# Depthwise convolution wholly on TensorE inside the first projection, with DMA-delayed copies

## The chip, the cores and the metric

The kernel runs on one core of one Trainium2 chip. The metric is device time in microseconds (us) of one execution, lower being better; several executions give a median. A core has TensorE (PE, matmuls), VectorE (DVE), ScalarE (ACT) and GpSimd (POOL), each working through its own instructions in order, and SyncE (SP), which here issues the loads. ACT and POOL can issue transfers too. All transfers share 16 DMA engines.

## The reference

Two layers of a streaming encoder on one sequence of 256 tokens, width 2048, in float32. Each layer has a token mixer (a Conformer convolution module in layer 0, gated linear attention in layer 1) and then a conv-FFN of hidden width 5632. Shift, scale and gate of every sub-layer come from a vector c by a projection (adaLN).

```python
mod = (silu(c) @ ada_w[i] + ada_b[i]).reshape(B, 6, 1, D)
h = rms_norm(x, norm_g[i, 0]) * (1.0 + scale_m) + shift_m
# layer 0's mixer:
a, gate = split(h @ w_in, 2)
z = causal_dwconv(a * sigmoid(gate), dw_w, dw_b)      # 31 taps per channel
y = silu(layer_norm(z, ln_g, ln_b)) @ w_out
x = x + gate_m * rms_norm(y, norm_g[i, 1])
```

The six parts of mod are numbered m = 0 to 5: shift, scale and gate of the mixer, then of the FFN. The change touches layer 0's mixer and the adaLN work that runs beside it.

## The kernel before, in words

**Weights.** All weights arrive as 1 MB blocks (128 partitions by 2048 numbers) in the order of one list, `items`, through a class `Stream`. It issues the loads on SP's queue, up to eight items ahead (L92 to L99), into two pools of four buffers: `raw` for weights and `cols` for the adaLN blocks marked early. A weight block is split into a high part in a reduced float format (hi, on ACT, L121) and the remainder (lo, on DVE, L123), in halves of 1024 columns. Each product is then three matmuls: hi by high input, hi by low input, lo by high input.

**adaLN blocks.** A block comes in one of two forms. A column block (`ada_col`, L353) is multiplied with silu(c) on PE: four float32 matmuls of 512 columns, in four column tiles of 32 beside each other, which the profile shows as eight records a block. After four blocks DVE transposes the sums and small matmuls with a mask add the four partial sums (adas, L378). A row block (`ada_row`, L347) holds the same matrix transposed, and one DVE instruction multiplies it with cb, silu(c) on all partitions, and adds up along the row (L350). The tables `ADA`, `COLS_CONV`, `COLS_COUT` and `ROWS_COUT` say after which weight block how many adaLN blocks stand in the list.

**The mixer's first half** (`conv_mixer`, L597 on). The projection runs in six steps (`STEPS`), each over some input tiles and some of the 16 output blocks j of 128 channels, since input tiles become ready only as shift and scale arrive. Numbered from 1: steps 5 and 6 are the last ones, for which all input tiles are ready; step 5 completes blocks 0 to 7, two for each weight block, and step 6 completes blocks 8 to 15, one each. `gather` (L658) adds up the steps' sums in the tile pair (L665), and once a block is complete takes the gate's sigmoid on ACT (L668) and multiplies (L671).

**The convolution.** Eight blocks are convolved on DVE, one instruction for each of 30 taps (`taps_dve`, L685). The other eight, `PE_BLOCKS`, go to PE (`taps_pe`). There the four 32-channel groups of a block are copied with delays of 0 to 3 frames into a tile zr by matmuls with pieces of the identity (ps_late, L713) and copies on ACT (L715). Then 8 times 4 matmuls with 32 by 32 diagonals, held in a tile zt, give the 31 taps (L730); zt is built by a DVE product (L724) and by 16 ACT instructions (L728). The function `conv` hands out both kinds in small portions after the projection, with early column blocks between them (the loop with `early_cols`). `mean_add` and `squares` sum blocks for the layer norm by matmuls with ones (acc_m, L644; acc_v, L633).

**Layer norm and the second half.** The variance is turned into r_ln on DVE and ACT (L778 to L786), all 16 blocks are centred (L789), then scaled, passed through Silu and split (L792 to L796). `proj_out` multiplies by the output weights in four quarters of 512 columns (ps_cout, L525 to L527). Its evacuation multiplies by the gate, which `gate_rows` writes to DRAM as one row and reads back on all partitions, on POOL's queue (L511, L515). The gate's m = 2 has to be complete for that. m = 3 and 4 are wanted by the FFN behind it.

## Time and profile before

| | us |
|---|---|
| median of three runs | 2382.68 (2380.72 to 2386.43) |
| the profiled execution | 2384.22 |
| its span, first to last instruction | 2382.5 |
| PE busy in the span | 2326.0 |
| DVE busy | 1776.0 |
| ACT busy | 1225.2 |
| the output projection's first matmul starts at | 371.17 |

The span runs from the first to the last instruction of the profiled execution. Times inside it count from its start. A group of instructions is named by line, engine, operation and the tiles that it writes and reads. A release such as "<-DMA raw<-in_adac" names what the engine waited for last.

### The profile page before, as it was taken

The page shows a single profiled execution, that of the slowest core. Times are in us where ns is not written, and L with a number is a line of the kernel's source. Part 1 is how long each engine was busy: PE and PEld are TensorE (multiplying, and loading weights), DVE is VectorE, ACT ScalarE, POOL GpSimd, SP SyncE. Part 2 cuts the span into 40 slices and gives each one's busy share as a digit, 9 for nine tenths or more (in the row PEclk, how much of TensorE's full clock was granted, in tenths as well). Part 3 has the DMA queues.
Part 4 walks back from the last instruction along what each step waited for, and adds up shares of the span by engine and source line. Part 5 has one row for each costly group of instructions (what it writes and reads, how often), then busy time and mean ns, then how long its engine had stood idle before and what let it go on. Part 6 is the DMA issues. An engine that isn't in the chain of part 4 may idle for free.

```text
span 2382.5 us, 34222 instructions
## 1 busy us (share of the span) xinstructions
PE 2326.0 (98%) x13522; PEld 1957.6 (82%) x13522; DVE 1776.0 (75%) x2522; ACT 1225.2 (51%) x1941; POOL 16.7 (1%) x43
## 2 busy tenths in 40 slices
...
GB/s 385 342 312 300 303 245 296 261 206 280 281 306 358 303 287 302 364 290 298 350 166 259 287 213 228 164 228 109 289 288 264 198 192 194 186 187 195 193 200 118
DMA packets 86578, 609.31 MB, mean 256 GB/s; under 512 B 10064, under 2 KB 10128, under 8 KB 13456
## 3 DMA queue, kind: packets, MB, share of 16 engines
...
HBM read 604.94 MB, written 2.13 MB: 255 GB/s over the span
## 4 chain that ended last, share of the span: by engine, by line
PE 95%; DMA 2%; ACT 1%; DVE 1%; issue 0%; SPq 0%; DVEq 0%; ACTq 0%
PE ps_fb L410 14%; PE ps_fa L410 14%; PE ps_fa L412 7%; PE ps_fb L412 7%; PE ps_fo L526 6%; PE ps_fo L527 6%; PE ps_fo L525 6%; PE ps_cin L756 3%; PE ps_cin L758 3%; PE ps_cin L757 3%; PE ps_r L410 2%; PE ada L364 2%; PE ps_r L412 1%; PE ps_q L410 1%; PE ps_cout L525 1%; PE ps_k L410 1%
## 5 line engine op out<-in xcount | busy, mean ns | idle before, releaser
L123 DVE TENSOR_TENSOR lo<-raw,hi 128x1024 fp32r<-128x1024 f32 (+1 forms) x760 | 914.0, 1214 | 392.0 <-ACT hi L121 388.6
L121 ACT CAST hi<-raw 128x1024 fp32r<-128x1024 f32 (+1 forms) x760 | 784.2, 1042 | 802.9 <-PE ps_fa L410 187.3
L410 PE MATMUL ps_fa<-h,hi 128*128 128x512 f32 x1408 | 358.6, 393 | 1.0 <-ACT h L486 0.9
L410 PE MATMUL ps_fb<-h,hi 128*128 128x512 f32 x1408 | 357.2, 392 | 0.0
L350 DVE CUSTOM_DVE_ANT_0 raw<-raw,cb 128x2048 f32<-128x2048 f32 x140 | 319.6, 2285 | 28.8 <-DMA raw<-in_adar 28.4
L410 PEld LDWEIGHTS ps_fa<-h,hi 128*128 128x128 f32 x1408 | 253.6, 189 | 46.8 <-issue 1.2
L410 PEld LDWEIGHTS ps_fb<-h,hi 128*128 128x128 f32 x1408 | 253.6, 189 | 44.2
L526 PE MATMUL ps_fo<-lo,u 128*128 128x512 f32 x704 | 274.7, 390 | 3.6 <-DVE lo L123 3.6
L527 PE MATMUL ps_fo<-hi,u 128*128 128x512 f32 x704 | 274.5, 390 | 0.0
L525 PE MATMUL ps_fo<-hi,u 128*128 128x512 f32 x704 | 273.9, 390 | 0.0
L412 PEld LDWEIGHTS ps_fa<-h,lo 128*128 128x128 f32 x1408 | 194.1, 190 | 14.9 <-DVE lo L123 0.5
L412 PEld LDWEIGHTS ps_fb<-h,lo 128*128 128x128 f32 x1408 | 193.8, 190 | 14.1
L412 PE MATMUL ps_fa<-h,lo 128*128 128x256 f32 x1408 | 198.9, 282 | 0.1
L412 PE MATMUL ps_fb<-h,lo 128*128 128x256 f32 x1408 | 198.2, 282 | 0.0
L526 PEld LDWEIGHTS ps_fo<-lo,u 128*128 128x128 f32 x704 | 132.6, 188 | 31.4 <-DVE lo L123 4.0
L527 PEld LDWEIGHTS ps_fo<-hi,u 128*128 128x128 f32 x704 | 132.6, 188 | 27.7
L525 PEld LDWEIGHTS ps_fo<-hi,u 128*128 128x128 f32 x704 | 132.5, 188 | 27.3
L756 PE MATMUL ps_cin<-h,hi 128*128 128x256 f32 x512 | 147.1, 291 | 6.1 <-ACT hi L121 6.1
L758 PE MATMUL ps_cin<-h,lo 128*128 128x256 f32 x512 | 144.6, 288 | 2.3 <-DVE lo L123 2.3
L757 PE MATMUL ps_cin<-h,hi 128*128 128x256 f32 x512 | 145.9, 288 | 0.4 <-DVE h L491 0.4
L756 PEld LDWEIGHTS ps_cin<-h,hi 128*128 128x128 f32 x512 | 99.3, 195 | 18.5 <-ACT hi L121 8.8
L757 PEld LDWEIGHTS ps_cin<-h,hi 128*128 128x128 f32 x512 | 99.6, 195 | 5.6 <-DVE h L491 4.7
...
## 6 DMA issues: line engine op xcount, KB each, us to landing
raw<-in_fin SPq DMA_DIRECT2D x176, 1024.0 KB, 4.8
raw<-in_adar SPq DMA_DIRECT2D x140, 1024.0 KB, 6.0
raw<-in_fout SPq DMA_DIRECT2D x88, 1024.0 KB, 5.6
raw<-in_adac SPq DMA_DIRECT2D x44, 1024.0 KB, 6.1
raw<-in_gin SPq DMA_DIRECT2D x33, 1024.0 KB, 4.9
raw<-in_cin SPq DMA_DIRECT2D x32, 1024.0 KB, 11.0
raw<-in_cout SPq DMA_DIRECT2D x16, 1024.0 KB, 7.2
raw<-in_gv SPq DMA_DIRECT2D x16, 1024.0 KB, 4.8
```

What stands on the lines that cost most here:

```text
L121: nc.scalar.copy(hi[:, :w], r[:, s : s + w])
L123: nc.vector.tensor_sub(lo[:, :w], r[:, s : s + w], hi[:, :w].bitcast(F32))
L350: V.tensor_tensor_reduce(out=r, in0=r, in1=cb, scale=1.0, scalar=0.0, op0=ALU.mult, op1=ALU.add, accum_out=mod[l, m][:, k : k + 1])
L364: nc.tensor.matmul(ps[32 * (j % 4) : 32 * (j % 4) + 32], cz[:, kt], r[:, j * n : (j + 1) * n], start=kt < 4, stop=kt >= KT - 4, tile_posit ...
L410: nc.tensor.matmul(ps, hi(k * P), act[k], start=k == 0, stop=False)
L412: nc.tensor.matmul(ps[:, :T], lo(k * P), act[k][:, :T], start=False, stop=k == nk - 1)
L525: nc.tensor.matmul(pv, ah, wh, start=kt == 0, stop=False)
L526: nc.tensor.matmul(pv, ah, wl, start=False, stop=False)
L527: nc.tensor.matmul(pv, al, wh, start=False, stop=kt == nk - 1)
L756: nc.tensor.matmul(ps[:, b], hi(o), ah, start=k == 0, stop=False)
L757: nc.tensor.matmul(ps[:, b], hi(o), al, start=False, stop=False)
L758: nc.tensor.matmul(ps[:, b], lo(o), ah, start=False, stop=k == nk - 1)
```

## The change

All 16 blocks are convolved on PE, inside projection steps 5 and 6. When a block is complete, `gather` writes it to DRAM from POOL's queue and reads it back four times, delayed by 0 to 3 frames, straight into one of three zr tiles. The delaying matmuls and the ACT copies go, and so do the DVE taps. `conv` now does one whole block; it is called as soon as more than `LAG` = 2 blocks wait. Both halves of zt are built on DVE.

The adaLN list changes: of m = 2 only 4 blocks stay columns and of m = 4 only 8 (`COLS`), the rest become row blocks; 25 of these stand inside the projection, where 12 column blocks stood, and four column blocks (`gap_cols`, where 16 stood in the tail) lie at its end, ahead of the output weights. In the output projection stand 8 column and 11 row blocks (4 and 16 before). Column blocks there are ordered behind a matmul of the output projection, row blocks of layer 0 behind the layer norm.

The start loads in another order: column blocks between the halves of x, cb behind the first weight block, part of the parameters early by ACT's queue and the rest late, the taps in step 3 and half as many. The layer norm becomes one fixed line of DVE instructions with high priority, in which each block's product, low part and the centring of a later block alternate, and the Silu table is loaded only after the root.

What moves, on three engines. First PE at the end of the projection, before: the last projection matmuls (ps_cin), a column block (ada), the mean sums (acc_m), then the delaying matmuls (ps_late) and diagonals (ps_conv) of the first block for PE.

```order
1616 L757 MATMUL ps_cin_15_2789<-h_15_1828,hi_1024_2720 128x256
1617 L758 MATMUL ps_cin_15_2789<-h_15_1828,lo_1024_2721 128x256
1618 L364 MATMUL ada_2630<-raw_2470,cz 32x512 x4
1619 L644 MATMUL acc_m_2867<-pair_301,ones 128x256
1620 L644 MATMUL acc_m_2867<-pair_316,ones 128x256
1621 L713 MATMUL ps_late_0_2872<-zp_176,ident 32x284 x4
1622 L713 MATMUL ps_late_1_2878<-zp_176,ident 32x284 x4
1623 L713 MATMUL ps_late_2_2884<-zp_176,ident 32x284 x4
1624 L713 MATMUL ps_late_3_2890<-zp_176,ident 32x284 x4
1625 L730 MATMUL ps_conv_2896<-zr,zt 32x256 x8
```

Now the first convolution stands in step 5, between the projections of blocks 2 and 3 (ps_cin_2, ps_cin_3), and PE comes to it directly after block 2.

```order
1093 L719 MATMUL ps_cin_2_2001<-h_15_1842,hi_0_1905 128x256
1094 L720 MATMUL ps_cin_2_2001<-h_15_1842,hi_0_1905 128x256
1095 L721 MATMUL ps_cin_2_2001<-h_15_1842,lo_0_1906 128x256
1096 L694 MATMUL ps_conv_2036<-zr_181,zt 32x256 x32
1097 L719 MATMUL ps_cin_3_2074<-h_12_1822,hi_1024_1909 128x256
1098 L720 MATMUL ps_cin_3_2074<-h_12_1822,hi_1024_1909 128x256
1099 L721 MATMUL ps_cin_3_2074<-h_12_1822,lo_1024_1910 128x256
1100 L719 MATMUL ps_cin_3_2074<-h_13_1827,hi_1024_1909 128x256
```

So PE cannot go on to block 3 before block 0's zr has landed. Second POOL's queue at that place, now (before, it issues nothing there): the writes of blocks 0 and 1 (zd, from pair), the four reads of each into zr, then the write of block 2.

```order
16 L678 DMA zd_1942<-pair_305 128x256 [waits DVE_49]
17 L678 DMA zd_1977<-pair_320 128x256 [waits DVE_49]
18 L680 DMA zr_181<-zd_1942 32x4x256 [waits DMASW0_49,Pool_49]
19 L680 DMA zr_181<-zd_1942 32x4x255
20 L680 DMA zr_181<-zd_1942 32x4x254
21 L680 DMA zr_181<-zd_1942 32x4x253
22 L680 DMA zr_182<-zd_1977 32x4x256 [waits DMASW1_49,Pool_49]
23 L680 DMA zr_182<-zd_1977 32x4x255
24 L680 DMA zr_182<-zd_1977 32x4x254
25 L680 DMA zr_182<-zd_1977 32x4x253
26 L678 DMA zd_2030<-pair_335 128x256 [waits DMASW2_49,DVE_49]
```

The reads wait for the write's landing (DMASW), and a later block's write stands behind an earlier block's reads. Third DVE in step 5, before: the additions of blocks 0 to 2 (pair from ps_cin), two low parts, the gate products (pair from g), and then taps.

```order
168 L665 TENSOR_TENSOR pair_301<-pair_301,ps_cin_0_1897 128x512
169 L665 TENSOR_TENSOR pair_316<-pair_316,ps_cin_1_1927 128x512
170 L123 TENSOR_TENSOR lo_0_1975<-raw_1706,hi_0_1974 128x1024
171 L123 TENSOR_TENSOR lo_1024_1979<-raw_1706,hi_1024_1978 128x1024
172 L671 TENSOR_TENSOR pair_301<-pair_301,g 128x256
173 L671 TENSOR_TENSOR pair_316<-pair_316,g 128x256
174 L665 TENSOR_TENSOR pair_331<-pair_331,ps_cin_2_1982 128x512
175 L685 SCALAR_TENSOR_TENSOR pair_301<-pair_301,tp 128x255
```

And now, at the same place:

```order
179 L669 TENSOR_TENSOR pair_305<-pair_305,ps_cin_0_1913 128x512
180 L669 TENSOR_TENSOR pair_320<-pair_320,ps_cin_1_1948 128x512
181 L355 ISA raw_1720,m_105<-raw_1720,cb 128x2048
182 L355 ISA m_105 128x1
183 L675 TENSOR_TENSOR pair_305<-pair_305,g 128x256
184 L675 TENSOR_TENSOR pair_320<-pair_320,g 128x256
185 L669 TENSOR_TENSOR pair_335<-pair_335,ps_cin_2_2001 128x512
186 L355 ISA raw_1722,m_105<-raw_1722,cb 128x2048
```

A row block (raw with cb) stands ahead of the gate product that the first write to DRAM waits for.

The diff, cut to what the prediction speaks of:

```diff
-PE_BLOCKS = (5, 7, 9, 11, 12, 13, 14, 15)
-NA = 12
+LAG = 2
+NA = 10
...
-ADA = ((2, 1, 1, 0), (3, 3, 2, 0), (1, 1, 1, 1, 1, 1, 1, 1), (3, 3, 2, 0), (1,) * 4, (1,) * 8)
-COLS_CONV = 16
+ADA = ((2, 1, 1, 0), (3, 3, 2, 0), (1, 1, 2, 1, 2, 1, 2, 1), (3, 3, 2, 0), (2, 3, 3, 2), (2, 2, 2, 2, 2, 1, 1, 0))
+COLS = {2: (0, 4), 4: (8, 16)}
...
-COLS_COUT = (0, 0, 0, 1), (1, 1, 1, 1), (1, 1, 0, 0), (0, 0, 0, 0)
-ROWS_COUT = (0, 0, 0, 4), (2, 1, 2, 1), (2, 1, 2, 1), (0, 0, 0, 0)
+COLS_COUT = (0, 0, 0, 0), (1, 1, 1, 1), (1, 1, 1, 1), (0, 0, 0, 0)
+ROWS_COUT = (0, 0, 0, 1), (1, 1, 2, 1), (2, 1, 1, 1), (0, 0, 0, 0)
...
+    pr = const.tile([P, NPAR], F32, tag="pr", name="pr")
+    A.dma_start(out=pr[:, :C_DWB], in_=par[:, :C_DWB])
...
-    cols += [(0, m, k, 4, i) for m in (2, 4) for k in range(0, KT, 4) for i in range(4)]
-    rows += [(0, 3, k) for k in range(KT)]
+    cols += [(0, m, k, 4, i) for m in (2, 4) for k in range(*COLS[m], 4) for i in range(4)]
+    rows += [(0, m, k) for m in (2, 3, 4) for k in range(KT) if m == 3 or not COLS[m][0] <= k < COLS[m][1]]
...
-            for _ in range(ADA[s][i]):
-                if ada:
+            for a in range(ADA[s][i]):
+                if ada and (s < 2 or s == 3 or s == 2 and a == 0):
                     put(ada.pop(0))
                 else:
-                    fillc(1)
-    early_cols = list(cols[:COLS_CONV])
-    fillc(COLS_CONV)
+    gap_cols = list(cols[:4])
+    fillc(4)
...
     def ada_row(key, r):
         _, l, m, k = key
-        V.tensor_tensor_reduce(out=r, in0=r, in1=cb, scale=1.0, scalar=0.0, op0=ALU.mult, op1=ALU.add,
-                               accum_out=mod[l, m][:, k : k + 1])
+        with tc.issue_after(apool["ln"].ins) if "ln" in apool and l == 0 else ExitStack():
+            V.tensor_tensor_reduce(out=r, in0=r, in1=cb, scale=1.0, scalar=0.0, op0=ALU.mult, op1=ALU.add,
+                                   accum_out=mod[l, m][:, k : k + 1])
...
-                             start=kt < 4, stop=kt >= KT - 4, tile_position=(0, 32 * (j % 4)))
+            with tc.issue_after(apool["tok"].ins) if "tok" in apool else ExitStack():
+                nc.tensor.matmul(ps[32 * (j % 4) : 32 * (j % 4) + 32], cz[:, kt], r[:, j * n : (j + 1) * n],
+                                 start=kt < 4, stop=kt >= KT - 4, tile_position=(0, 32 * (j % 4)))
         if i == KT // per - 1:
...
     for t in range(2):
+        st.load(t + 2)
         for c in range(4):
             nc.sync.dma_start(out=X[t][c], in_=x[t, :, c * 512 : (c + 1) * 512])
-    nc.sync.dma_start(out=pr, in_=par)
-    st.load(4)
+    st.load(5)
+    nc.sync.dma_start(out=cb, in_=cvec.to_broadcast([P, D]))
+    nc.sync.dma_start(out=pr[:, C_DWB:], in_=par[:, C_DWB:])
...
-            nc.sync.dma_start(out=tp, in_=taps)
+            tp = cm.tile([P, KT, 4, 8], F32, tag="tp", name="tp", bufs=1)
             ss = new_sums("in")
+            for zr in zrs:
+                G.memset(zr, 0.0)
...
+                    for i in added[len(squared) :][: 3 if n < KT - 1 else KT]:
                         squares(i)
...
             def gather(j, ps, last):
...
                     V.tensor_mul(zp, zp, g)
+                    zr = zrs[j % 3]
+                    zd = dram.tile([4, 32, T], F32, tag="zd", name=f"zd{j}", bufs=3)
+                    G.dma_start(out=zd.rearrange("b n t -> (b n) t"), in_=zp)
+                    for i in range(4):
+                        G.dma_start(out=zr[32 * i : 32 * i + 32, :, 28 + i :], in_=zd.rearrange("b n t -> n b t")[:, :, : T - i])
+                    on_pe.append(j)
...
-            def taps_dve():
...
-                            V.scalar_tensor_tensor(z[:, s:], zp[:, : T - s], tap(j, s), z[:, s:], ALU.mult, ALU.add)
-                            yield None
-                    for j, _, _ in two:
-                        yield j
...
-            def taps_pe():
...
-                        pr4 = pp["ps"].tile([P, 512], F32, tag="ps", name=f"ps_late{j}_{b}")[:, : 28 + T]
-                        for i in range(4):
-                            nc.tensor.matmul(pr4[32 * i : 32 * i + 32], ident[:, 32 * b : 32 * b + 32], zp[:, 4 - i : 32 + T - i],
-                                             start=True, stop=True, tile_position=(0, 32 * i))
-                        A.copy(zr[:, b], pr4)
-                        yield None
...
-                            else:
-                                for b in range(16):
-                                    A.activation(zt[:, b // 4, b % 4], mask32, AF.Copy, scale=w[:, a + b // 4, b % 4 : b % 4 + 1])
...
+            def conv():
...
+                j = on_pe.pop(0)
+                ps = pp["ps"].tile([P, 2 * T], F32, tag="ps", name=f"ps_conv{j}")[:, :T]
+                for a in range(8):
+                    if a % 4 == 0:
+                        zt = cm.tile([P, 4, 4, 32], F32, tag="zt", name="zt", bufs=2)
+                        V.tensor_mul(zt, tp[:, j, :, a : a + 4].rearrange("p b a -> p a b").unsqueeze(3).to_broadcast([P, 4, 4, 32]),
+                                     mask32.unsqueeze(1).unsqueeze(1).to_broadcast([P, 4, 4, 32]))
                     for b in range(4):
+                        nc.tensor.matmul(ps[32 * b : 32 * b + 32], zt[:, a % 4, b], zrs[j % 3][:, b, 28 - 4 * a : 28 - 4 * a + T],
+                                         start=a == 0, stop=a == 7, tile_position=(0, 32 * b))
+                A.activation(zs[j], ps, AF.Identity, bias=pc(C_DWB + j))
+                return j
...
             for s, (k0, nk, j0, j1) in enumerate(STEPS):
+                if s == 2:
+                    nc.sync.dma_start(out=tp.rearrange("p j b a -> p (j b a)"), in_=taps)
...
                         gather(j, ps, k0 + nk == KT)
-                    if k0 + nk == KT:
-                        conv(dve, taps_dve, 8)
+                        if len(on_pe) > LAG:
+                            z = conv()
+                            for i in done:
+                                mean_add(i)
+                            done[:] = [z]
...
-            for step in range(1000):
-                if step < len(early_cols):
-                    st.upto(("col",) + early_cols[step], False)
-                if len(added) == KT:
-                    break
-                late, ready[:] = list(ready), []
...
-                conv(pe, taps_pe, 7)
-                conv(dve, taps_dve, 8)
+            st.prepare(2)
+            while on_pe:
+                z = conv()
...
+                done[:] = [z]
...
-            V.scalar_tensor_tensor(part_a, acc["m"], 1.0 / D, part_a, ALU.mult, ALU.add)
-            V.tensor_add(mu, mean_a, part_a)
-            A.activation(part_a, part_a, AF.Square)
-            V.scalar_tensor_tensor(r, acc["v"], 1.0 / D, part_a, ALU.mult, ALU.subtract)
-            V.tensor_scalar_max(r, r, 0.0)
-            A.activation(r, r, AF.Sqrt, bias=epsb)
-            V.reciprocal(r, r)
-            warm(AF.Silu, acc["v"])
-            for j in range(KT):
-                V.tensor_sub(zs[j], zs[j], mu)
...
+            line = []
+            def queue(f, *args):
+                with tc.issue_after(line[-1].ins) if line else ExitStack():
+                    line.append(f(*args))
+            def center(j):
+                if j < KT:
+                    queue(V.tensor_sub, zs[j], zs[j], mu)
+            def low(j):
+                if j >= 0:
+                    queue(V.tensor_sub, us[j][:, T:], zs[j], us[j][:, :T].bitcast(F32))
+            with tc.high_priority(SPLIT_FIRST):
+                queue(V.scalar_tensor_tensor, part_a, acc["m"], 1.0 / D, part_a, ALU.mult, ALU.add)
+                queue(V.tensor_add, mu, mean_a, part_a)
+                A.activation(part_a, part_a, AF.Square)
+                queue(V.scalar_tensor_tensor, r, acc["v"], 1.0 / D, part_a, ALU.mult, ALU.subtract)
+                queue(V.tensor_scalar_max, r, r, 0.0)
+                A.activation(r, r, AF.Sqrt, bias=epsb)
+                warm(AF.Silu, r)
+                for j in range(3):
+                    center(j)
+                queue(V.reciprocal, r, r)
+                for j in range(KT):
+                    queue(V.tensor_mul, zs[j], zs[j], r)
+                    A.activation(zs[j], zs[j], AF.Silu, bias=pc(C_LNB + j), scale=pc(C_LNG + j))
+                    us.append(hpool.tile([P, 2 * T], F32R, tag="h", name=f"uc{j}"))
+                    A.copy(us[j][:, :T], zs[j])
+                    low(j - 2)
+                    center(j + 3)
+                low(KT - 2)
+                low(KT - 1)
+            st.upto(("col",) + gap_cols[-1], False)
...
```

101 lines of the change are left out of this document (23 added, 78 removed).

## The prediction

> **What bounds the kernel now.** I read the page first. TensorE (PE) is busy for 98% of the span, so a change counts where it takes work off PE's queue or closes one of PE's few gaps.
>
> ```profile
> PE 2326.0 (98%) x13522; PEld 1957.6 (82%) x13522; DVE 1776.0 (75%) x2522; ACT 1225.2 (51%) x1941; POOL 16.7 (1%) x43
> ```
>
> Next a table of the first layer's mixer by stretch. Its columns are the stretch, its length, the busy time of PE, weight loads, DVE, ACT and POOL, PE's clock, the DMA share and GB/s.
>
> ```profile
> 0.00:30.00 30.00, 10.34 (x89) 5.01 (x89) 5.16 (x19) 14.96 (x36) 1.50 (x12) 0.98 0.95 379
> 30.00:185.00 155.00, 150.03 (x1240) 132.16 (x1241) 110.96 (x142) 61.35 (x84) 0.00 (x0) 0.97 0.84 344
> 185.00:269.80 84.80, 84.80 (x708) 72.62 (x707) 77.14 (x152) 36.48 (x53) 0.00 (x0) 1.00 0.73 291
> 269.80:356.10 86.30, 86.14 (x1048) 48.34 (x1048) 83.38 (x209) 51.17 (x184) 1.33 (x1) 1.00 0.76 268
> 356.10:371.20 15.10, 1.97 (x9) 0.31 (x9) 15.10 (x39) 7.46 (x14) 2.14 (x4) 0.62 0.61 158
> 371.20:462.00 90.80, 90.33 (x408) 71.58 (x409) 76.25 (x85) 46.51 (x71) 0.00 (x0) 0.99 0.86 334
> ```
>
> These are the start, projection steps 1 to 4, steps 5 and 6, the convolution tail, layer norm, and the output projection. PE idles 20 us in the start and 13 us in layer norm, and is full nearly everywhere else. Third, the chain of waits in order of time (start, length, what), which tells what holds those two places.
>
> ```profile
> 26.96 0.84 ACT zt L728 x4
> ...
> 28.92 0.94 ACT hi L121
> ...
> 29.91 0.58 PE ps_cin L756
> ...
> 199.12 0.99 PE ada L364 x8
> ...
> 318.75 3.16 PE ps_conv L730 x56
> 321.91 0.86 PE ada L364 x8
> ...
> 355.06 1.01 PE ada L364 x4
> 356.08 13.10 DMA raw<-in_adac
> 369.23 1.94 PE ada L364 x8
> 371.17 0.73 PE ps_cout L525
> ```
>
> The first projection matmul waits for a weight cast (hi) that stands on ACT behind diagonals for a convolution that comes 240 us later (zt). The gap ahead of the output projection is booked to a late adaLN block.
>
> **Start.** Three transfers no longer stand ahead of the first weight block:
>
> ```profile
> cb<-in_cvec ACTq DMA_DIRECT2D x1, 1024.0 KB, 4.8
> ...
> tp<-in_taps SPq DMA_DIRECT2D x1, 504.0 KB, 11.5
> pr<-in_par SPq DMA_DIRECT2D x1, 366.0 KB, 5.6
> ```
>
> They hold 1.9 MB, of which about 0.16 MB of parameters stay early: 1.8 MB at the 379 GB/s of the first row of the table is 4.7 us. The zt work on ACT goes as well (0.84 us on the chain and a little more). I take -6. The bounds are 0, since the second half of x now comes behind three column blocks and may end last, and -8.
>
> **Column blocks out of the projection.** Twelve of them leave PE between projection blocks, at 0.99 us each (the row at 199.12), with three sums of about 0.3: -13. Row blocks on DVE replace them. These groups price that and what follows (line, engine, operation, shapes, count, busy time, mean ns):
>
> ```profile
> L123 DVE TENSOR_TENSOR lo<-raw,hi 128x1024 fp32r<-128x1024 f32 x96 | 113.7, 1219 | 18.6 <-ACT hi L121 18.6
> ...
> L350 DVE CUSTOM_DVE_ANT_0 raw<-raw,cb 128x2048 f32<-128x2048 f32 x28 | 63.7, 2283 | 0.0
> ...
> L665 DVE TENSOR_TENSOR pair<-pair,ps_cin 128x512 f32<-128x512 f32 x56 | 38.0, 684 | 31.0 <-PE ps_cin L758 30.7
> ...
> L644 PE MATMUL acc_m<-pair,ones 128*128 128x256 f32 x32 | 9.3, 408 | 0.0
> L633 PE MATMUL acc_v<-sq,ones 128*128 128x256 f32 x32 | 8.8, 401 | 0.1
> ...
> L671 DVE TENSOR_TENSOR pair<-pair,g 128x256 f32<-128x256 f32 x16 | 6.7, 421 | 0.0
> L668 ACT ACTIVATE g<-pair 128x256 f32<-128x256 f32 x16 | 6.5, 414 | 15.0 <-DVE pair L665 15.0
> ...
> L724 DVE TENSOR_TENSOR zt<-tp,mask 128x512 f32<-128x512 f32 x8 | 5.4, 680 | 0.0
> ...
> L515 POOL DMA_DIRECT2D gs<-row x4 | 2.1, 542 | 15.0 <-ACT pair L793 15.0
> ```
>
> DVE loses all its taps. Over steps 5 and 6 it then has 24 low parts of 1.22, 16 additions of 0.68, 16 products of 0.42, 28 diagonal tiles of 0.68, 22 row blocks of 2.28 and a few squares, some 125 us of the 150 that these steps will take. In step 5 alone there is no such room: 8 low parts of 1.22, 8 additions of 0.68, 8 products of 0.42, 12 diagonal tiles of 0.68 and 10 row blocks of 2.28 make 49.6 us. PE has there four weight blocks, six convolutions of 3.75 (below) and five mean sums of about 0.6. A weight block is 5.94 us, from its first matmul to the next column block:
>
> ```profile
> 234.84 0.38 PE L756 MATMUL ps_cin<-h,hi 128*128 128x256 f32 x1
> ...
> 240.78 1.07 PE L364 MATMUL ada<-raw,cz 128*32 128x512 f32 x8
> ```
>
> That is 49.3 us on PE, so every wait between the two engines in step 5 shows.
>
> **The convolutions.** Each of 16 blocks is 64 matmul records (512 for 8 before); 56 take 3.16 us (row at 318.75), so a block is 3.61. Set between projection matmuls it changes PE's tiling twice. The eight adaLN matmuls take 0.99 there and 0.86 between convolutions, which do not change it: 0.13 a block, so 3.75 and 60 in all. The Trainium skill, "TensorEngine Tiling (Array Packing)", Key Properties, says that a change of tiling mode drains TensorE, which speaks against this change; the two rows bear it out, but small, and weaving would cost 2 us. With 18.1 us of mean and variance sums (L644, L633) and four column blocks kept for the gap (4.2 with their sums) PE has 82.3 us where the tail took 86.3: -4.
>
> **Layer norm.** The gap of 15.1 us goes down to its own chain. Its parts in the profile of before, on ACT and then on DVE:
>
> ```profile
> 355.91 1.28 ACT L785 ACT_TABLE_LOAD   x1
> 357.20 0.51 ACT L785 ACTIVATE r_ln<-r_ln,epsb 128x256 f32<-128x256 f32 x1
> ```
>
> ```profile
> 359.40 1.75 DVE L786 RECIPROCAL r_ln<-r_ln 128x256 f32<-128x256 f32 x1
> ```
>
> Table load, root and reciprocal make 3.5 us; two DVE steps ahead, and product, Silu, copy behind, at 0.4 to 0.5 each, make 2.3; some eight hand-overs add 1 to 1.5. That is 7.5, so -7.6. The 13.1 us wait for a column block goes only because the gap's four blocks now load ahead of six weight blocks; if they were late again, 5 us come back.
>
> **Output projection.** Four more column blocks run in it, and one sum: +4.3. Layer norm now hands its 16 tiles over while the first quarter runs, three DVE steps of about 0.34 each, beside six low parts of 1.22: 24 us of DVE against 90.8/4 = 22.7 of PE. I take +2. The gates' row (m = 2) is now complete only with the gap's column blocks, where POOL wrote it well ahead before:
>
> ```profile
> 349.51 1.33 POOL L511 DMA_DIRECT2D row<-m  x1 [347.38 <-DVE m L508]
> ```
>
> Transfers by the issuing queue, with KB each and us from issue to landing:
>
> ```profile
> g<-row POOLq DMA_DIRECT2D x12, 256.0 KB, 6.9
> ...
> out_dram<-x SPq DMA_DIRECT2D x8, 256.0 KB, 2.2
> ...
> row<-m POOLq DMA_DIRECT2D x4, 8.0 KB, 15.7
> ```
>
> The row's write (15.7 us) and the copies back (6.9) start about 4 us ahead of the output projection and end about 20 us into it. The first quarter's evacuation on DVE wants them at 22.7. I cost this at nothing, covered by that quarter; without cover it is up to 5 us, since low parts queue behind that product.
>
> **Copies.** Each block of the convolution now waits for one write to DRAM and four reads back, all on POOL's queue. The write waits for the gate product on DVE, the reads for the write's landing, and the next block's write stands behind them. No such copy is in the trace. The nearest rows are the three above.
>
> A write and the reads lie between 2.2 (an undisturbed write from SBUF) and 6.9 (four reads at once on POOL's queue beside weight loads); 15.7 is for single numbers and is nearest to neither. I take 4.5 for both, the middle. For the first block: addition 0.7, gate 0.4, a row block standing ahead of the product on DVE 2.3, product 0.4, two write issues of 0.54, landing 4.5, four read issues 2.2, landing 4.5 make 16 us. PE covers about 4 of it with what is left of blocks two and three, so it stands 12 us, once. Later blocks of step 5 have two half weight blocks, two convolutions and two sums ahead of them (14.6 us) against about the same chain, and step 6 has 20; I add 2 for all. That is +14. With 2.2 for both it is 7 in all. With 6.9 for both the first wait is 17, and POOL needs 0.54 + 6.9 + 2.2 = 9.6 us a block where PE's pace in step 5 is 7.3, another 14 over six blocks, and 2 at the end: 33. The Trainium skill, "DMA: Bandwidth & Descriptors", Anatomy of one DMA, gives 2.0 us and the bytes at 436 GB/s, an estimate of 2.3 for the write and 3.2 for the four reads together; by it the copies would cost about 8, and the sum would be near -16.
>
> **Sum.** -6 - 13 - 4 - 7.6 + 4.3 + 2 + 14 = -10.3 us against the profiled execution's 2384.2 (its span of 2382.5 and 1.7 around it), or 2373.9. The median of the runs is 1.5 lower, so 2372.4.
>
> **Rivals.** *The copies hide.* With 2.2 us landings the sum is -17: 2366. For it: POOL is idle (16.7 us in the span) and DMA has a quarter free in steps 5 and 6. Against it: the first block still has nothing in front of it.
>
> *POOL's copies become the bound, and it is slower.* Place: the waits of the convolutions for zr in step 5. It decides from copy costs above 10.3 + 14 = 24.3 us, which is at landings of about 6. With 6.9, as in the g row, the sum is +9: 2391. With 15.7 for the write a block holds POOL 18 us, 16 blocks 295 us where PE has about 150: +120 or more. For it: that row is on the same queue, under the same loads. Against it: it moves twice the bytes per transfer.
>
> *DMA fills up.* Step 5 carries four weight blocks and ten row blocks (14.7 MB) and eight blocks of copies (0.655 MB each): 19.9 MB in 49.3 us plus the first wait. At 344 GB/s, the rate of steps 1 to 4, that is 58 us, which the waiting time of 12 holds almost. If copies cost double for their short rows, it is 73 us, 12 more than I have: +2, 2385.
>
> **How the numbers follow.** About 0.2%, 4.8 us, is what a measurement of this kernel can tell from no change. Forecast 0.50, copies hide 0.22, POOL bounds 0.17, DMA fills 0.11. Of the forecast's own spread (-6 of start or of layer norm may fail) 0.05 falls within 0.2%, the rest is faster. Faster 0.67, same 0.05 + 0.11 = 0.16, slower 0.17. The range reaches from start and copies both at their good ends (-20, less some 6 for what I book twice or not at all, -26) to copies that cost 30, or to a late gate row and late column blocks beside copies of 20 (+5.7 either way): 2356 to 2388.
>
> **What would show it.** In the profile after: the first ps_cin near 24; steps 5 and 6 about 150 us with 14 convolutions inside; one wait of PE for zr of about 12 us at the first ps_conv, and few later; output projection starting about 17 us earlier, and some 7 us of PE idle ahead of it; POOL's writes landing in 3 to 6 us. Waits for zr at every convolution, or PE waiting for row blocks on DVE, would make it wrong.

## The result, and the profile after

The changed kernel takes 2421.0 us (median of 4 runs, 2419.3 to 2422.6), the kernel before 2383.8 beside it: a ratio of 1.0156, 95% interval 1.0139 to 1.0174. It is slower by 37.2 us; the prediction was 10 us faster, with a range that ended at 2388. The profiled execution took 2421.1 us, its span 2419.0, against 2382.5 before.

Nearly all of it is lost in the first layer. A few first and last matmuls cut the span of both profiles into the same places (the first ps_cin, the last ps_h of step 4, the first ps_cout, the first ps_fa of the FFN):

| place | before, us | after, us | change | predicted |
|---|---|---|---|---|
| start, to the first ps_cin | 29.9 | 26.9 | -3.0 | -6 |
| steps 1 to 4 | 148.7 | 153.1 | +4.5 | 0 |
| steps 5, 6, convolutions, layer norm | 192.6 | 210.4 | +17.8 | -13 - 4 - 7.6 + 14 = -10.6 |
| output projection | 106.2 | 124.5 | +18.3 | +6.3 |
| the rest | 1905.1 | 1904.1 | -1.0 | 0 |

The page of after has PE's share down from 98% to 96%, with the same work on it (2324.0 us against 2326.0):

```profile
PE 2324.0 (96%) x13538; PEld 1960.5 (81%) x13538; DVE 1744.1 (72%) x2333; ACT 1189.7 (49%) x1775; POOL 63.5 (3%) x124
```

The table by stretch of after shows where PE stands still. Its columns are as in the prediction (stretch, length, busy PE, weight loads, DVE, ACT, POOL, PE's clock, DMA share, GB/s); the stretches are the beginning of step 5, its remainder with the beginning of step 6, the remainder of step 6, layer norm, and the output projection up to 480 in three pieces. Between the third and the fourth lie the convolutions left over, in which PE is full.

```profile
180.70:230.00 49.30, 28.83 (x275) 23.83 (x274) 37.58 (x47) 12.02 (x18) 8.94 (x16) 0.79 0.90 321
230.00:280.00 50.00, 39.39 (x408) 29.41 (x405) 35.09 (x41) 9.18 (x14) 10.97 (x20) 0.86 0.97 316
280.00:345.00 65.00, 58.73 (x655) 47.13 (x654) 41.28 (x54) 21.68 (x33) 16.46 (x30) 0.97 0.79 259
...
384.30:390.40 6.10, 0.49 (x16) 0.32 (x16) 5.58 (x14) 3.13 (x6) 1.17 (x1) 0.89 0.99 345
390.40:420.00 29.60, 29.59 (x119) 24.25 (x120) 29.06 (x56) 24.73 (x45) 2.17 (x4) 0.91 0.54 183
420.00:450.00 30.00, 30.00 (x163) 20.18 (x162) 22.41 (x25) 8.52 (x11) 0.00 (x0) 1.00 0.94 346
450.00:480.00 30.00, 21.79 (x107) 14.21 (x105) 18.68 (x20) 9.09 (x12) 0.00 (x0) 0.85 0.95 386
```

From 180.7 to 345 PE is idle for 37 us, and its clock is below 1 in the same stretches. DVE has room there (73 us busy of 99 up to 280), POOL too; only DMA is near full (0.90 and 0.97 up to 280). Layer norm is down to 6.1 us, as forecast. Between 450 and 480 PE loses 8 us more. PE's waits in the first 600 us (what waits, for what, us in total, times, longest) name the causes:

```profile
PE ps_conv L694 <- DMA zr<-zd: 35.2, 7, 18.3
...
PE adas L384 <- DVE adat L377: 6.6, 5, 3.6
PE ps_cin L721 <- DVE lo L123: 5.9, 6, 2.5
...
PE ps_cout L534 <- ACT hi L121: 4.5, 1, 4.5
...
PE ps_cout L534 <- ACT uc L774: 3.9, 1, 3.9
```

Convolutions wait for their copies seven times, 35.2 us in all. Two of these waits, the first and the third, in the chain of waits of after (start, length, what):

```profile
196.68 0.69 DVE pair L669
197.36 2.20 DVE raw L355
199.57 0.35 DVE pair L675
...
200.22 5.08 DMA zd<-pair
...
205.91 1.38 POOL zr L680 x3
...
207.57 10.09 DMA zr<-zd
...
217.79 5.62 PE ps_conv L694 x64
...
229.34 9.05 DMA zd<-pair
...
240.60 8.05 DMA zr<-zd
```

The links are those that the prediction named, a row block ahead of the product on DVE among them; the landings are not. They are 5.08, 10.09, 9.05 and 8.05 where it took 4.5. The list of transfers has their medians (KB each, us from issue to landing):

```profile
zd<-pair POOLq DMA_DIRECT2D x16, 128.0 KB, 6.3
zr<-zd POOLq DMA_DIRECT2D x16, 128.0 KB, 6.3
...
zr<-zd POOLq DMA_DIRECT2D x16, 127.5 KB, 7.7
```

The blocks of PE behind such waits, with the wait in brackets, show a second cost:

```profile
217.79 5.62 PE L694 MATMUL ps_conv<-zr,zt 128*32 128x256 f32 x64 [18.28 <-DMA zr<-zd]
...
237.60 5.96 PE L694 MATMUL ps_conv<-zr,zt 128*32 128x256 f32 x64 [4.03 <-DMA zr<-zd]
...
260.20 6.59 PE L694 MATMUL ps_conv<-zr,zt 128*32 128x256 f32 x64 [4.26 <-DMA zr<-zd]
...
293.91 5.12 PE L694 MATMUL ps_conv<-zr,zt 128*32 128x256 f32 x64 [3.03 <-DMA zr<-zd]
...
308.63 3.66 PE L694 MATMUL ps_conv<-zr,zt 128*32 128x256 f32 x64 [3.24 <-DMA zr<-zd]
```

A block of 64 takes 3.66 us, but behind the three waits of 4.03 us and more it takes 5.62 to 6.59, and behind the one of 3.03 it takes 5.12: 8.6 us more for the four together. The granted clock (the third number from the end) in stretches of 4 us behind four of these five waits says why:

```profile
217.00:221.00 4.00, 3.21 (x32) 1.79 (x36) 0.00 (x0) 0.00 (x0) 0.00 (x0) 0.50 1.01 269
237.00:241.00 4.00, 3.40 (x33) 1.83 (x37) 0.00 (x0) 0.00 (x0) 2.04 (x4) 0.50 1.00 415
...
294.00:298.00 4.00, 4.00 (x50) 2.20 (x54) 0.81 (x3) 0.42 (x1) 2.18 (x4) 0.64 0.86 300
...
308.00:312.00 4.00, 3.37 (x64) 2.38 (x64) 1.39 (x3) 0.00 (x0) 1.74 (x4) 1.00 0.35 131
```

After 4.03 us of idling PE runs at half its clock for some 4 us, after 3.24 us at all of it: 33 convolution matmuls run in that time against 64. But after 3.03 us it is slow as well, for part of the 4 us, so the length of a wait alone does not decide it here. The Trainium skill, "TensorE: Matmul & The Clock Gate", Part 1: The HAM clock gate, says that an idle window of about 3.4 us halves the clock until PE has been busy for about as long; the waits of 4.03 us and more and the one of 3.24 agree with that figure, the one of 3.03 does not.

In the output projection two waits of PE remain:

```profile
459.48 1.22 PE L534 MATMUL ps_cout<-hi,uc 128*128 128x512 f32 x2 [4.54 <-ACT hi L121]
...
478.92 0.29 PE L384 MATMUL adas<-adat,mask 128*32 128x2 f32 x8 [3.63 <-DVE adat L377]
```

The first is for a weight block that was asked for at 448.76 and landed 9.53 us later. SP, which issues the loads in order, had this to do (start, length, what):

```profile
384.26 0.33 SPq L97 DMA_DIRECT2D raw<-in_adac  x1
401.11 6.29 SPq L97 DMA_DIRECT2D raw<-in_cout  x2
...
448.34 0.33 SPq L97 DMA_DIRECT2D raw<-in_adar  x1
448.76 0.38 SPq L97 DMA_DIRECT2D raw<-in_cout  x1
```

From 384.6 to 401.1 it issues no load. The load that it stands at is a weight block's, and it goes out 0.03 us after the low part of an earlier output weight has ended on DVE (at 401.08), which gives a weight buffer back. From 420 on DMA works at 0.94 and 0.95. The late weight itself stands directly behind a row block's load (448.34) that goes out 0.02 us after a column block has ended on PE (at 448.32) and given back a buffer of the adaLN blocks.

### The profile page after: what moved, and what is told of

Same layout as the page of the kernel before. It is cut to its first block, busy times and chain, and to the rows that moved or that the text cites. A ratio compares the mean times of both kernels' runs of the same rounds, so it can differ in the third digit from the quotient of the medians.

```text
span 2419.0 us, 34059 instructions
## 1 busy us (share of the span) xinstructions
PE 2324.0 (96%) x13538; PEld 1960.5 (81%) x13538; DVE 1744.1 (72%) x2333; ACT 1189.7 (49%) x1775; POOL 63.5 (3%) x124
## 4 chain that ended last, share of the span: by engine, by line
PE 91%; DMA 4%; DVE 2%; ACT 1%; issue 1%; POOL 0%; SPq 0%; DVEq 0%; ACTq 0%; POOLq 0%
PE ps_fb L417 13%; PE ps_fa L417 13%; PE ps_fa L419 7%; PE ps_fb L419 7%; PE ps_fo L535 6%; PE ps_fo L536 6%; PE ps_fo L534 6%; PE ps_r L417 2%; PE ps_cin L721 2%; PE ps_cin L719 2%; PE ps_cin L720 2%; PE ps_conv L694 2%; DMA zr<-zd 2%; PE ps_cout L534 1%; PE ps_r L419 1%; PE ps_cout L535 1%
## 5 line engine op out<-in xcount | busy, mean ns | idle before, releaser
L355 DVE CUSTOM_DVE_ANT_0 raw<-raw,cb 128x2048 f32<-128x2048 f32 x160 | 365.2, 2284 | 35.9 <-DMA raw<-in_adar 35.6
L419 PEld LDWEIGHTS ps_fa<-h,lo 128*128 128x128 f32 x1408 | 194.1, 190 | 14.9 <-DVE lo L123 0.5
## 6 DMA issues: line engine op xcount, KB each, us to landing
raw<-in_cin SPq DMA_DIRECT2D x32, 1024.0 KB, 11.4
```

The costliest lines, as they stand in the source:

```text
L355: V.tensor_tensor_reduce(out=r, in0=r, in1=cb, scale=1.0, scalar=0.0, op0=ALU.mult, op1=ALU.add, accum_out=mod[l, m][:, k : k + 1])
L419: nc.tensor.matmul(ps[:, :T], lo(k * P), act[k][:, :T], start=False, stop=k == nk - 1)
```

## The experiments

My theory was that the copies' landings are long because row blocks, weight blocks and copies share full DMA engines (traffic), that PE's waits and the slow clock behind them follow from that, and that the output projection loses by loads that are held back. The rivals: POOL's queue, which holds the writes behind the reads; row blocks on DVE, ahead of the gate products; the order within layer norm. All times stand beside 2384 to 2385 for the kernel before.

### The copies, alone

**No copies.** The five transfers of each block are left out, so a convolution reads the zeros that zr was set to.

```diff
                     zr = zrs[j % 3]
-                    zd = dram.tile([4, 32, T], F32, tag="zd", name=f"zd{j}", bufs=3)
-                    G.dma_start(out=zd.rearrange("b n t -> (b n) t"), in_=zp)
-                    for i in range(4):
-                        G.dma_start(out=zr[32 * i : 32 * i + 32, :, 28 + i :], in_=zd.rearrange("b n t -> n b t")[:, :, : T - i])
```

> The write to DRAM and the four reads of every block are left out; the convolutions multiply zeros, so the convolution's result is left out too. Everything else of the changed kernel stays. If the copies are the loss, the 35.2 us of waits for zr go and the slow convolutions behind them (6.59 us instead of 3.66) go too, some 9 us: 2421 - 44 = 2377, with the output projection starting near 346. If the 124.5 us from the output projection's first matmul to the FFN's first one come from held-back loads and not from the copies, they stay near 124; if they are a consequence of the copies, they fall to about 112 and the time to 2365.

Measured: 2374.4 us, 0.9956 (0.9936 to 0.9976). The first ps_cout stands at 345.2 against 390.4 with copies, so the copies cost 45.2 us of PE's time there, 46.6 in all, as expected for this run; the prediction had 14. From the first ps_cout to the FFN it takes 123.5 us, against 124.5: that loss has nothing to do with the copies. In 230 to 280 PE is full, DVE is full too, and DMA moves more than with the copies (373 GB/s against 316):

```profile
230.00:280.00 50.00, 50.00 (x595) 39.86 (x588) 49.34 (x59) 15.61 (x22) 0.00 (x0) 1.00 0.97 373
```

**Copies that nothing waits for.** All copies run, but the convolutions read a tile of zeros, z0.

```diff
-                        nc.tensor.matmul(ps[32 * b : 32 * b + 32], zt[:, a % 4, b], zrs[j % 3][:, b, 28 - 4 * a : 28 - 4 * a + T],
+                        nc.tensor.matmul(ps[32 * b : 32 * b + 32], zt[:, a % 4, b], z0[:, 28 - 4 * a : 28 - 4 * a + T],
```

> All copies are made as before, but the convolutions read a tile of zeros and wait for none of them (the convolution's result is left out). Queue theory (a block holds POOL's queue for some 11 us, PE's pace is 7.3, and only the wait matters): as without copies, about 2377. Traffic theory (copies and row blocks fill the DMA engines, 0.97 busy from 230 to 280, and PE will wait for weights when it does not wait for zr): about half of the 44 us stay, 2395 to 2400, with waits for hi or lo in steps 5 and 6.

Measured: 2393.5 us, 1.0038 (1.0018 to 1.0058); the first ps_cout at 361.9. So copies cost 16.7 us even where no convolution waits for them. (They need not be a part of the 45.2: in the changed kernel PE's waits may hold the traffic back.) PE's waits have a line that neither kernel has:

```profile
PE ps_conv L695 <- DVE zt L692: 9.9, 6, 4.0
```

The row blocks land late now, DVE waits for them (three loads, raw<-in_adar, take 21.25 to 24.46 us in the chain), and the diagonals zt stand behind them on DVE. The copies themselves take longest here, 11.4 us for a write:

```profile
zd<-pair POOLq DMA_DIRECT2D x16, 128.0 KB, 11.4
```

**Writes on ACT's queue.** Then no write can stand behind reads that wait. The reads stay on POOL's queue.

```diff
-                    G.dma_start(out=zd.rearrange("b n t -> (b n) t"), in_=zp)
+                    A.dma_start(out=zd.rearrange("b n t -> (b n) t"), in_=zp)
```

> The write of each block goes out from ACT's queue instead of POOL's; the four reads stay on POOL, so a block's write no longer stands behind the reads of the block before. All is computed as in the reference. Queue theory (POOL serves one block after another, 11 us each, where PE's pace is 7.3): the waits after the first one shrink from 17 us to about 5 and the slow clock after them goes with it, 2400 to 2405. Traffic theory (transfers land late because the DMA engines are full, whatever the queue): no change, 2417 or more.

Measured: 2424.8 us, 1.0167 (1.0138 to 1.0196). Nothing is gained; PE waits 18.34, 8.54 and 7.89 us, and the landing is no shorter:

```profile
zd<-pair ACTq DMA_DIRECT2D x16, 128.0 KB, 7.1
```

So the theory that writes held behind reads on POOL's queue make the loss falls. The Trainium skill, "Trainium Kernel Development and Optimization", Key Constraints, says that the queues of SP, ACT and POOL run on the same 16 DMA engines and that several of them save only time of issuing; this run agrees.

### Room for the copies

**Rows not loaded.** The 22 row blocks of steps 5 and 6 are not loaded, and DVE multiplies the vector by itself in their place (bare marks these blocks).

```diff
-            self.nc.sync.dma_start(out=r[:, : it["n"]], in_=it["src"])
+            if not it["bare"]:
+                self.nc.sync.dma_start(out=r[:, : it["n"]], in_=it["src"])
...
-            V.tensor_tensor_reduce(out=r, in0=r, in1=cb, scale=1.0, scalar=0.0, op0=ALU.mult, op1=ALU.add,
+            V.tensor_tensor_reduce(out=r, in0=cb if key in no_load else r, in1=cb, scale=1.0, scalar=0.0, op0=ALU.mult, op1=ALU.add,
```

> The loads of the 22 row blocks of steps 5 and 6 are left out; DVE does the same 22 multiplications on other data (those parts of the gate and of the FFN's shift are left out). Copies, waits and order stay. Traffic theory: without these 23 MB the copies land in 2.5 to 3 us instead of 6 to 8, a block holds POOL some 6 us, and only the first convolution waits, about 10 us: near 2390. Queue theory with landings that belong to POOL's transfers themselves: landings stay at 6 or more, over 2410.

Measured: 2410.5 us, 1.0111 (1.0082 to 1.0141); the first ps_cout at 380.1. The landings fell to 4.8 us for a write and 2.6 to 2.9 for reads, but the time by only 10. The multiplications no longer waited for loads and ran ahead of the gate product, so the first write was issued at 209.3 instead of 200.2, and the first convolution still waited 12.9. The time is thus near what the rival had forecast, but the landings settle the question that the time leaves open. The first block's write, its reads and its convolution in the chain of this run, and the stretch of 200 to 210:

```profile
209.34 3.90 DMA zd<-pair
...
215.52 2.69 DMA zr<-zd
...
218.34 6.07 PE ps_conv L700 x64
```

```profile
200.00:210.00 10.00, 5.42 (x46) 5.22 (x44) 9.09 (x13) 5.05 (x6) 0.66 (x1) 0.98 0.13 39
```

From the write's issue to the convolution it takes 9.0 us, where it took 17.6 in the changed kernel, on the same queue and in the same order. DMA is 0.13 busy from 200 to 210, where it was 0.94 there.

**No rows at all.** As above, and the multiplication is cut to 8 elements.

```diff
-            V.tensor_tensor_reduce(out=r, in0=r, in1=cb, scale=1.0, scalar=0.0, op0=ALU.mult, op1=ALU.add,
+            n = 8 if key in no_load else D
+            V.tensor_tensor_reduce(out=r[:, :n], in0=(cb if key in no_load else r)[:, :n], in1=cb[:, :n], scale=1.0, scalar=0.0, op0=ALU.mult, op1=ALU.add,
```

> The 22 row blocks of steps 5 and 6 are left out altogether, loads and multiplications (those parts of the gate and of the FFN's shift are left out). Copies, waits and order stay. If row blocks are what makes the copies expensive, by traffic on the DMA engines (landings of 6 to 8 us) and by standing ahead of the gate product on DVE, then landings are at 2.5 to 5 us, the first convolution waits some 10 us, later ones next to nothing, and the output projection starts near 360: 2390. If POOL's queue alone is to blame, over 2405.

Measured: 2402.3 us, 1.0073 (1.005 to 1.0095); the first ps_cout at 370.3. The transfers of this run:

```profile
zd<-pair POOLq DMA_DIRECT2D x16, 128.0 KB, 5.9
zr<-zd POOLq DMA_DIRECT2D x16, 128.0 KB, 2.8
```

PE waits 14.0 us at the first convolution and only 3.0 more for another copy. The later waits go, with DMA busy for 0.66 instead of 0.97 of 230 to 280. The first one stays, and the chain shows that it is not the latency of idle engines:

```profile
202.07 11.55 DMA zr<-zd
```

```profile
200.00:210.00 10.00, 0.00 (x0) 0.00 (x0) 2.10 (x11) 0.42 (x1) 5.04 (x10) 0.58 1.00 317
```

Without the row blocks SP issued one weight block, three column blocks and a later row block between 199.1 and 203.3, and the first block's reads landed after 11.55 us among them. So copies come late here where DMA is full, whichever loads fill it. The time came out between the two expectations, 12 us above the lower.

**Convolutions one block later.** The lag between a block's projection and its convolution goes from 2 to 3. A fourth zr and half-size zt tiles go with it.

```diff
-LAG = 2
+LAG = 3
...
-            zrs = [cm.tile([P, 4, 28 + T], F32, tag=f"zr{i}", name=f"zr{i}", bufs=1) for i in range(3)]
+            zrs = [cm.tile([P, 4, 28 + T], F32, tag=f"zr{i}", name=f"zr{i}", bufs=1) for i in range(4)]
```

> Four zr tiles and a lag of three blocks instead of two (mu shares a tile with the mean, the diagonals are built in four tiles of half the size instead of two); all is computed as in the reference. Latency theory (each block's chain of some 18 us from product to landed reads is longer than the 14.6 us of work that a lag of two puts before it): with 22 us before it only the first convolution waits, about 12 us, near 2395. Queue theory (throughput: 11 us a block on POOL): the first wait falls by 6 us, but the later ones come back as POOL falls behind, 2410 to 2418.

Measured: 2410.6 us, 1.0107 (1.008 to 1.0135). The waits are 14.9, 2.7, 4.4 and 2.0; -10 us, and it is the fastest kernel with all copies and rows. The latency theory's 2395 was missed and the queue theory's 2410 met, but by the trace DMA is full (1.02 busy from 230 to 280) and the median write lands after 9.6 us.

**The lag of 3 and no rows**, the two edits together.

> The run without the 22 row blocks of steps 5 and 6 (2402.3), and a lag of three blocks with four zr tiles. Copies stay, on POOL. If the copies' cost that is left there is latency of the first block and its slow clock (14 us of waiting, PE at half clock behind it), a lag of three gives one half weight block more before it, 3 us less of waiting, and the few later waits go: 2393 to 2398. If POOL's throughput still binds without the row blocks: 2401 or more.

Measured: 2396.5 us, 1.0053 (1.0034 to 1.0071); the first ps_cout at 363.7. Two waits are left, 6.45 and 4.19 us. With a DMA share of 0.53 from 230 to 280 (1.03 still from 210 to 230) and one block more of lead this is still 18 us behind the kernel without copies (345.2, its rows in place), part of it the slow clock: the first convolution block behind the 6.45 us took 6.10.

**Rows in step 6 alone.** The row blocks of step 5 move to step 6, with the sum unchanged.

```diff
-ADA = ((2, 1, 1, 0), (3, 3, 2, 0), (1, 1, 2, 1, 2, 1, 2, 1), (3, 3, 2, 0), (2, 3, 3, 2), (2, 2, 2, 2, 2, 1, 1, 0))
+ADA = ((2, 1, 1, 0), (3, 3, 2, 0), (1, 1, 2, 1, 2, 1, 2, 1), (3, 3, 2, 0), (0, 0, 0, 0), (3, 3, 3, 3, 3, 3, 3, 1))
```

> The ten row blocks of step 5 move to step 6, which then has 22 instead of 12; nothing else changes and all is computed as in the reference. Traffic theory (row blocks beside the copies are what makes them late): step 5 then shows the waits of the run without rows, 14 us once and next to nothing after; step 6 has 8 + 22 blocks and eight copies in some 100 us, 350 GB/s, and some waits come back there: 2403 to 2410. If the place of the row blocks doesn't matter, since the same bytes have to pass before the output projection: 2418 or more.

Measured: 2418.4 us, 1.0145 (1.0125 to 1.0165), 2.6 less than after, which the traffic theory had put at 2403 to 2410. The waits only move (16.6, 3.1, 6.1, 1.1, 3.3, 2.0). But the edit hardly moved the loads: from 187 to 228 SP issued nine row blocks, where it was eight in the changed kernel, as loads go out up to eight items ahead. So the run does not test what row blocks beside the copies cost.

### Layer norm and the start

**Without the order behind layer norm.** Row blocks may run on DVE among its steps again.

```diff
-        with tc.issue_after(apool["ln"].ins) if "ln" in apool and l == 0 else ExitStack():
+        with ExitStack():
```

> Row blocks of layer 0 are no longer ordered behind the layer norm on DVE; nothing else. Theory of held-back loads for the output projection (row blocks keep their buffers until the layer norm's line is through, SP issues one load between 384.6 and 412, and the debt comes due in the wait of 4.5 us for a weight at 459): SP issues earlier, and the 124.5 us from first matmul to FFN fall to about 115, 2411. Rival (the four more column blocks and the layer norm's hand-over simply take that time): no change, or worse by the 2.28 us of each row block that now stands ahead of the layer norm, 2421 to 2428.

Measured: 2430.3 us, 1.0194 (1.0165 to 1.0224), 9 slower than after. The wait for the late weight is gone, but waits for layer norm's results are worse, the second of them inside the output projection, which took 125.6 us and not the 115 of the theory:

```profile
PE ps_cout L534 <- ACT uc L774: 8.4, 1, 8.4
...
PE ps_cout L536 <- DVE uc L747: 7.0, 1, 7.0
```

**The start alone, in the kernel before** (its order of loads, the parameters on ACT's queue, the taps later).

```diff
-    st.load(1)
     for t in range(2):
+        st.load(t + 2)
...
-    nc.sync.dma_start(out=pr, in_=par)
-    st.load(4)
+    st.load(5)
+    nc.sync.dma_start(out=cb, in_=cvec.to_broadcast([P, D]))
```

> The kernel before with the order of the start loads only (column blocks between the halves of x, cb and parameters behind the first weight block, taps in step 3); all is computed as in the reference. The first ps_cin came at 25.2 to 26.9 in the runs with it, at 29.9 before. If these 3 to 5 us stay to the end: 2380 to 2381, below both kernels. If the loads behind them set the pace, as in the run with the start and the layer norm, where 12.8 us gained by the output projection's start were gone at its end: 2384.

Measured: 2382.75 us, 0.9995 (0.9986 to 1.0004). The first ps_cin comes at 26.3 instead of 29.9; at the FFN 1.8 us of it are left, and at the end nothing that can be measured.

**Start and layer norm, in the kernel before**: the line of layer norm's steps, and column blocks put behind a matmul of the output projection.

```diff
+            def queue(f, *args):
+
+                with tc.issue_after(line[-1].ins) if line else ExitStack():
+                    line.append(f(*args))
...
+            with tc.issue_after(apool["tok"].ins) if "tok" in apool else ExitStack():
+                nc.tensor.matmul(ps[32 * (j % 4) : 32 * (j % 4) + 32], cz[:, kt], r[:, j * n : (j + 1) * n],
+                                 start=kt < 4, stop=kt >= KT - 4, tile_position=(0, 32 * (j % 4)))
```

> The kernel before with three parts of the change only: the order of the start loads (taps in step 3), layer norm as one fixed line of DVE instructions with the Silu table after the root, and column blocks of the output projection ordered behind one of its matmuls. Convolutions and adaLN lists stay as before; all is computed as in the reference. The start gave 3 us in the changed kernel (first ps_cin at 26.9 for 29.9), and its layer norm had PE idle for 6 us where before it was 15. If these parts hold by themselves: 2384 - 3 - 8 = 2373. If the late column block (13.1 us) is not cured by them, 2381. If the fixed line delays the low parts of the output weights, as in the changed kernel's output projection, 2385 or more.

Measured: 2388.25 us, 1.0015 (1.0005 to 1.0024). The gap did not close (15.8 us): a row block stood among the steps on DVE and waited 5.65 us for its load. From the first ps_cout to the FFN it takes 111.8 us.

**The same with the row blocks ordered behind layer norm**, as in the change.

```diff
+        with tc.issue_after(apool["ln"].ins) if "ln" in apool and l == 0 else ExitStack():
+            V.tensor_tensor_reduce(out=r, in0=r, in1=cb, scale=1.0, scalar=0.0, op0=ALU.mult, op1=ALU.add,
```

> The kernel before with the start loads, the fixed line of the layer norm, column blocks behind an output matmul, and now also row blocks of layer 0 ordered behind the layer norm; all is computed as in the reference. In the run without that last part four row blocks stood among the layer norm's steps on DVE, one of them with 5.7 us of waiting for its load, and PE idled 15.8 us. If that was the cause, PE idles 6 to 7 us there and the time is 2384 - 3 - 9 + 3 (the output projection took 5 us longer there) = 2375, below both kernels. If the layer norm's chain is as long by itself, 2385 or more.

Measured: 2387.9 us, 1.0016 (1.0006 to 1.0026). The gap is 6.3 us now and the first ps_cout comes at 358.4, 12.8 us earlier than before. From there to the FFN it takes 122.7 us instead of 106.2 before and 111.8 in the run above. SP issues no load from 348.0 to 368.5, and PE waits for a weight:

```profile
PE ps_cout L531 <- ACT hi L121: 7.0, 1, 7.0
```

So what layer norm gains is given back in the output projection, without copies or new convolutions in the kernel, and with only the 4 column blocks there that stood in it before.

### The output projection

**Five load buffers, no copies.** One more buffer of 1 MB, and loads one further ahead. The memory for it comes from leaving the copies out (zr shrinks to two tiles of zeros), so the run compares with the one without copies (2374.4).

```diff
-    st.cols = early.enter_context(tc.tile_pool(name="cols", bufs=4))
+    st.cols = early.enter_context(tc.tile_pool(name="cols", bufs=5))
...
-            st.ahead = 8
+            st.ahead = 9
```

> The run without copies, and in the room of the zr tiles a fifth buffer for adaLN blocks (the stream is allowed nine blocks ahead instead of eight). Without copies it was 2374.4, with 123.5 us from the output projection's first matmul to the FFN's first. Theory of held-back loads (the buffers are full while the layer norm runs, SP issues nothing, and the debt comes due as a late weight): a fifth buffer takes one more block of 1 MB ahead, 2.7 us at 380 GB/s, and the wait of 4.5 us and its slow clock shrink or go: 2367 to 2371. If the buffers are not what holds the loads back: 2373 to 2376.

Measured: 2368.1 us, 0.9936 (0.9921 to 0.9951). The weight is no longer late, and the output projection takes 116.4 us instead of 123.5. SP still issues no load from 342.0 to 356.5, as in the run without copies, so the standstill alone does not make the weight late.

**No copies, and no rows in the output projection** (its row blocks neither loaded nor multiplied).

```diff
+    cut[0] = True
     for c in range(4):
...
             fill(ROWS_COUT[c][i])
+    cut[0] = False
```

> The run without copies, and without the 11 row blocks among the output weights (that part of the FFN's scale and shift is left out as well). With copies, leaving these rows out took the wait for a weight at 459 away and 6.6 us off the output projection, but the convolutions took 4 us longer in that execution, so that the time stayed. Theory of late loads: without that disturbance the time falls by 6 to 8 us against the run without copies, 2366 to 2368. If the 6.6 us were by chance: 2374.

Measured: 2368.0 us, 0.9933 (0.9915 to 0.9951), with 116.8 us for the output projection and no late weight. Fewer loads and one more buffer do the same.

**No rows in the output projection, with the copies** (the same edit on the changed kernel).

> The 11 row blocks that stand among the output weights are left out, loads and multiplications (that part of the FFN's scale and shift is left out). From the output projection's first matmul to the FFN's first one it is 124.5 us in the changed kernel and 106.2 before. Theory of late loads (25 blocks of 1 MB in 93 us, the DMA engines 0.94 to 0.97 busy from 420 to 480, so that a weight comes 4.5 us late at 459): without 11 MB the wait goes, and its slow clock: 124 becomes 113 to 116, 2410. Theory of column blocks (their buffers come free only as PE reaches them, and SP's queue waits behind them, with or without row blocks): the wait stays, 120 or more, 2417.

Measured: 2419.35 us, 1.0149 (1.0129 to 1.0169). The output projection falls to 117.9 us, but the first ps_cout came 4 us later in the profiled execution (394.7), so the time hides it.

**Four columns fewer in the output projection**: the third quarter's four become row blocks on DVE.

```diff
-COLS = {2: (0, 4), 4: (8, 16)}
+COLS = {2: (0, 4), 4: (12, 16)}
...
-COLS_COUT = (0, 0, 0, 0), (1, 1, 1, 1), (1, 1, 1, 1), (0, 0, 0, 0)
-ROWS_COUT = (0, 0, 0, 1), (1, 1, 2, 1), (2, 1, 1, 1), (0, 0, 0, 0)
+COLS_COUT = (0, 0, 0, 0), (1, 1, 1, 1), (0, 0, 0, 0), (0, 0, 0, 0)
+ROWS_COUT = (0, 0, 0, 3), (1, 1, 2, 2), (2, 1, 2, 1), (0, 0, 0, 0)
```

> Of m = 4 only four blocks stay columns instead of eight; the output projection gets 4 column and 15 row blocks (0, 0, 0, 3 / 1, 1, 2, 2 / 2, 1, 2, 1 rows), the projection as in the changed kernel. All is computed as in the reference. Theory of column blocks: the wait for a weight at 459 and the wait of 3.6 us for the sums of the last four column blocks (PE behind transposes and low parts on DVE) go with the four columns: 124 becomes 110 to 113, 2409. Theory of late loads: as many megabytes, so only the columns' own 4 us go, 2417.

Measured: 2419.8 us, 1.0151 (1.013 to 1.0171). The wait for the sums is gone, the late weight is not (3.3 us, and 1.9 for its low part). The output projection takes 119.7 us, 4.8 less; the stretches ahead of it and behind it came out 0.8 and 1.1 longer, so the span is 2416.1 against 2419.0 and the median nearly the same.

## Why the prediction was wrong

**Copies: +14 was +45.** This is the step that failed most. Its mechanism, one long first wait from product, write, issue, and read, was right; three numbers were not. The first wait was 18.3 us and not 12: reads of the first block landed after 10.09 us. Six further waits made 16.9 and not 2. And the slow clock, which the sum did not have, cost 8.6 on the convolution blocks. These make 43.8 of the 45.2. I had taken landings of 4.5, the middle between 2.2 beside no loads and 6.9 beside loads. The copies run beside loads, so the row for that case was the one to take: the medians were 6.3 to 7.8. With 6.9 the sum gave 33 for the copies, the case of the rival on POOL's copies; the clock was still missing.

**"DMA fills up" was the right rival with two fifths of its price.** It put 12 on top of the 14, since it counted only bytes against bytes; 31 came on top. The loss showed in latency: at 0.97 busy from 230 to 280 the median read of 128 KB landed after 6.3 us, at 0.66 after 2.8, and PE waits with it. That full engines make the landings long, and not POOL's queue, rests on the first block, which POOL served in the same order in three kernels: 17.6 us from its write's issue to its convolution with DMA at 0.94 from 200 to 210, and 9.0 with DMA at 0.13, while its reads alone took 11.55 where DMA was at 1.00 without any row block of steps 5 and 6. Writes on another queue changed nothing; the reads were never moved off POOL. Row blocks are behind most of the later waits (16.9 us with them, 6.9 without their loads, 3.0 without loads and multiplications), but the first wait came without them too. They pay as well: with nothing waiting for copies 16.7 us were lost, since the loads of row blocks, and with them DVE, came late.

**Convolutions -4 and columns -13: right together.** A block takes 3.66 us where the clock is full (predicted 3.61, or 3.75 with the change of tiling). In the kernel without copies, steps 5 to layer norm take 163.9 us against 192.6 before: -28.7, where the prediction without its copies had -24.6, layer norm's -7.6 among them. No run took these terms one by one.

**Start -6: it was -3 and didn't last.** The loads taken out of the way were worth 3.6 us in the run of the start alone, not the 4.7 of their bytes, and the work on ACT no more than that; what holds the remainder was not tested. By the FFN 1.8 were left. **Steps 1 to 4, put at nothing: +4.5.** Three more row blocks of 2.28 us stand on DVE there (15 against 12), and PE waits longer for low parts (lo) and h. PE's waits between 30 and 179 us of before had these two lines:

```profile
PE ps_cin L758 <- DVE lo L123: 2.3, 1, 2.3
PE ps_cin L757 <- DVE h L491: 0.4, 1, 0.4
```

After, it is 5.9 for lo, in six waits, and 2.5 for h. No run took these row blocks away alone. I had added up DVE's work for step 5 and not for step 3.

**Layer norm -7.6: right at its place, then given back.** PE idles some 6 us, as forecast. But a weight comes late behind it, which costs 7 us with the slow clock that follows (123.5 to 116.4, by one buffer more). That the order of the row blocks brings it about rests on the pair in the kernel before: with the order PE waits 7.0 us for a weight and the output projection takes 122.7 us, without it no weight is late and it takes 111.8, though there the loads also had 9 us more of layer norm to catch up. I had costed this order at nothing, since DVE and PE lose nothing by it; the loads do. Which buffers hold them back is not settled: the standstill ends with a weight buffer, the late weight stands behind a row block's load that waits for an adaLN buffer, and a fifth adaLN buffer cures the weight but not the standstill.

**Output projection +6.3: +18.3.** Of it 7 are that weight. How the other 11 divide is not shown: the predicted 6.3 for four columns and a slower first quarter, and the wait of 3.63 for a column's sums with the half clock behind it, would fill them, but the kernel before lost 16.5 us with the new start, layer norm and order alone, without the four columns. The run with four columns fewer took columns and sums together, for 4.8. The gates' row, which I worried about, was covered as said: its copies back were issued from 398.2 on and no wait of PE for them shows.

What stays open: how much of the 45 us a better order of the loads could recover with all copies and rows in place. The lag of 3 gained 10. A fifth load buffer beside the copies was not tried; its memory is taken by zr. No version with the whole computation was measurably faster than the kernel before.
